# One quad's weight loads on ScalarE's queue, loads and casts in another order, three loads pinned

## The chip, the cores and the metric

The kernel runs on one core of one Trainium2 chip. The metric is the device time in microseconds of one execution. The core has five engines with an instruction stream each: TensorE (PE in the profile, with its weight loads as PEld), VectorE (DVE), ScalarE (ACT), GpSimd (POOL) and SyncE (SP). SP here does nothing but issue DMAs; POOL and ScalarE can issue DMAs among their other work. A DMA's data are moved by the core's 16 DMA engines.

## The reference

```python
def reference(x, w1, w2):          # x 8 x 1024 x 1024, w1 1024 x 4096, w2 4096 x 1024, all float32
    h = x @ w1
    h = 0.5 * h * (1 + np.tanh(np.sqrt(2 / np.pi) * (h + 0.044715 * h ** 3)))
    return (h @ w2).astype(np.float32)
```

It is two matrix products with a gelu between them.

## The kernel before

The 8192 rows of x are taken as eight superblocks (numbered 0 to 7) of 1024 rows. In each, `g = gelu(x w1)` is computed and kept on the chip in float16, and then `g w2`.

Each of the two products is done by Strassen's method in Winograd's form: operands are cut into 2 x 2 blocks named "11", "12", "21", "22", seven products of blocks or of sums of blocks are computed instead of eight, and the results are added up. In superblocks 2 to 7 the method is used on two levels, so that one of the seven products is itself seven smaller ones. Products are numbered 1 to 7. Those of the weights that are plain blocks are 1, 2 and 3 (`W_TERM`); 5, 6, 7 and 4 are sums (`SUMS`). Names like "s7" are the inner sums of product 7.

**Superblocks 0 and 1** make the weights ready for all others. `matmul1` (L531) multiplies with one level, from `MadeQuad` objects (L189), each a quarter of w1's columns. In superblock 0 a quad is cast from w1 and written to DRAM (`w1_d`, L115). In superblock 1 it is loaded back from `w1_d` in four loads of 512 KB (L198, blocks 12, 11, 22, 21), and its sums are made on DVE (`sum`) and stored by POOL (L243). `product` (L501) calls `multiply` (L496), whose matmuls carry L497. `matmul2_made` (L840) does the second product, with matmuls at L1124, and makes, splits and stores w2's blocks and sums (`w2_d`, `in_d`). At the end of superblock 0's call it also transposes x's next superblock by DMA (`x_transpose`, L482, 16 transposes on SP, shown as L162), stores w2's block 22 (`keep("22")`, four stores on SP) and makes superblock 1's first `MadeQuad`.

**Superblocks 2 to 7** run `matmul1_late` (L774) and `matmul2` (L1142).

- `matmul1_late` goes through eight iterations j (called pairs) of 11.1 us, with an order of work written out by hand (`PAIR`, L30); its matmuls carry L712. A pair's weights come from a `StoredHalf` (L268): one load of 512 KB for each entry of `GROUPS` (L27, the loads carry L284), each holding two things that lie side by side in DRAM, for example products 1 and 5 together, or product 7 with its inner sums.
- The same loop brings in the next superblock's rows of x. In pairs 0 to 3 `x_cast_paced` (L475) has POOL copy a few elements of the current g (the "pace" copy, L477) and then issue two DMAs (L472) that cast 128 rows each from float32 to float16 in DRAM. In pairs 4 to 7 SP issues four DMA transposes each: blocks "22" and "21" (rows 512 to 1023) first, then "12" and "11" (rows 0 to 511).
- `matmul2` takes the seven products one after another as `Inner` objects (L1017), in the order 4, 1, 2, 5, 6, 7, 3 (L1194). Its matmuls carry L1082. Each `Inner` loads seven pieces of w2 (`load`): raw pieces from `w2_d` (L1038) and inner sums from `in_d` (L1034). Near the end, at products 7 and 3, the next superblock's first two `StoredHalf` objects are made, and their loads go out.

**What sets the order.** A scheduler places instructions on each engine. Matmuls, most copies and sums and a part of the DMAs are pinned (`keep_in_program_order`, for DMAs through `load_in_order`, L161) and keep the order of the program among each other. An unpinned load may be placed earlier, as soon as its tile is free. All loads from DRAM and the transposes stand in one queue, SP's, and what waits there holds up what is behind it. Most of them use tiles of the pool `up` (24 buffers); the tile names `mu` (pool `mp`, 2 buffers) and `xi` (one buffer) are two others, which come free at other times. SP's DMAs signal through eight completion counters in turn, so a DMA is issued only once the one eight places before it has landed.

Of the kernel before, what the change touches and what calls it, by code (L numbers as in the profile page):

```python
# [23 lines left out]
SUMS = tuple(W_SUM)  # L24
BLOCKS = ("11", "21", "12", "22")
STEPS = (1, 2, 6, 5, 7, 3, 4)
GROUPS = ((1, 5), ("s1", "s5"), (2, "s2"), (7, "s7"), (3, "s3"), (6, 4))  # L27
MADE_HALF = 3
ROOM = (("11", 4), ("11", 8), ("11", 12), ("22", 4), ("22", 8), ("22", 12), ("21", 4), ("21", 8), ("21", 12))
PAIR = """  # L30
m26' h41' z31' q1' r1' x77 v0' m11 s1' m15 x35 x36 z22' u1' X57' c1 m36' m35' m32' X76' m51 e30'
# [41 lines left out]
def kernel(  # L73
# [7 lines left out]
    nc = tc.nc  # L81
# [19 lines left out]
    up = ctx.enter_context(tc.tile_pool(name="up", bufs=24))  # L101
    gp = ctx.enter_context(tc.tile_pool(name="gp", bufs=1))
    gcp = ctx.enter_context(tc.tile_pool(name="gcp", bufs=4))
    mp = ctx.enter_context(tc.tile_pool(name="mp", bufs=2))
    xip = ctx.enter_context(tc.tile_pool(name="xip", bufs=1))
# [11 lines left out]
        for q in range(NI // QC)  # L117
        for n, ks in enumerate(GROUPS + (("12",),))
    }
    in_d = {m: dram.tile([P, 4, NI // 2, OH // 2], DT, name=f"in_d{m}") for m in range(1, 8)}  # L120
# [5 lines left out]
    term = {b: m for m, b in W_TERM.items()}  # L126
# [7 lines left out]
    def unit(rows, cols):  # L134
        return up.tile([P, rows, cols], DT, name="u")
# [6 lines left out]
    def w1_at(q, key):  # L142
        for (at, ks), d in w1_d.items():
            if at == q and key in ks:
                return d[:, :, ks.index(key), :]
# [4 lines left out]
    def halves(t):  # L150
        return t.rearrange("p (h k) n -> p h (k n)", h=2)
# [9 lines left out]
    def load_in_order(out, in_, **kw):  # L161
        return tc.keep_in_program_order(nc.sync.dma_start(out=out, in_=in_, **kw))  # L162
# [26 lines left out]
    class MadeQuad:  # L189


        def __init__(self, q, first, store):
            self.q, self.first, self.store = q, first, store
            self.raw = {b: unit(2 * KH, 2 * P) for b in BLOCKS}
            self.ops = {m: self.raw[b] for m, b in W_TERM.items()}
            if not first:
                for b in ("12", "11", "22", "21"):
                    nc.sync.dma_start(out=halves(self.raw[b]), in_=w1_at(q, term.get(b, b)))  # L198

        def load(self):  # L200

# [66 lines left out]
    class StoredHalf:  # L268


        def __init__(self, i, room=()):
            q, h = divmod(i, 2)
            self.ops, self.sums = {}, {}
            self.room = list(room)
            for ks in GROUPS:
                two = None
                if ks != ("s1", "s5"):
                    two = self.two(ks)
                    if ks == (1, 5):
                        self.both = two  # L280
                elif 0 < i < MADE_HALF:
                    two = self.two(ks)
# [75 lines left out]
    def x_blocks():  # L358
        return {b: unit(KH, HT) for b in ("22", "21", "12", "11")}
# [107 lines left out]
    def x_cast(s, after, rows=range(0, SB, P), xb=None):  # L467
        if xb is None:
            xb = xdram.tile([SB, H], DT, name="xb")
        with tc.issue_after(after.ins):  # L470
            for q in rows:
                nc.gpsimd.dma_start(out=xb[q:q + P, :], in_=x2[s * SB + q:s * SB + q + P, :])  # L472
        return xb

    def x_cast_paced(s, g_chunk, q, xb, pin=False):  # L475

        mark = nc.gpsimd.tensor_copy(out=pace, in_=g_chunk[:, :2])  # L477
        if pin:
            tc.keep_in_program_order(mark)
        return x_cast(s, mark, range(q * P, (q + 2) * P, P), xb)  # L480
# [293 lines left out]
    def matmul1_late(xs, sb, quads, g):  # L774
        n = NI // 2
        nxt = {}
        early = Inner(4, g["22"])
        made = set(xs.inner)
        last = None
        for j in range(n + 1):  # L780
            if j < n:
                quads += [StoredHalf(i) for i in range(len(quads), min(j + 3, n))]
                now = Pair(j, quads[j], xs, g)
            for key in PAIR:
                late = key.count("'")
                key = key.rstrip("'")
                if key[0] in "xX":
                    if late == j and int(key[1]) not in made:
                        xs.inner_sum(int(key[1]), int(key[2]), nc.vector if key[0] == "x" else nc.gpsimd)
                elif key == "b":  # L790
                    if 4 <= j < n:
                        early.make_quarter(7, j - 4)
                elif key[0] == "r":
                    if j == n - 1 + late:
                        early.make_quarter(6, int(key[1]))
                elif key[0] == "k":
                    if MADE_HALF <= j + 1 < n:
                        quads[j + 1].make(int(key[1]))
                elif late:
                    for i in BEGIN.get(key, ()) if j == n else ():  # L800
                        early.begin(i)
                    if last is not None:
                        last.run(key)
                elif j < n:
                    now.run(key)
            last = now
            if j == n:
                break
            if j == n - 1:
                early.load(STEPS[:3])  # L810
            if sb < NSB - 1:
                if j < 4:
                    nxt["xb"] = x_cast_paced(sb + 1, g["22"][:, 2 * j, :], 2 * j, nxt.get("xb"), True)
                if j == 3:
                    nxt["blocks"] = x_blocks()
                if j > 3:
                    x_transpose(nxt["xb"], load_in_order, nxt["blocks"], range(j - 4, j - 3))
        blocks = nxt.get("blocks")
        return g, early, None if blocks is None else XOps(blocks)
# [20 lines left out]
    def matmul2_made(sb, g, keep_w1, xb):  # L840
# [24 lines left out]
        def keep(b):  # L865
            if sb == 0:
                for q in range(NI // QC):
                    load_in_order(w2_at(q, term.get(b, b)), raw[b][q])
# [19 lines left out]
        s2, a, p5, t6, at = {}, {}, {}, {}, {}  # L888
# [47 lines left out]
        for m, name, first in (  # L936
            (1, "a", True), (2, "b", True), (5, "c", True), (6, "a", False),
            (3, "c", False), (7, "a", False), (4, "a", False),
        ):
            for q in range(NQ):  # L940
                if first:
                    banks[name].append(psum())
                bank = banks[name][q]
                matmuls2(bank, s2[q] if m == 6 else rows(g[operands[m]], q), pieces(m), first)
                post(m, q, bank)
                if (m, q) == (5, 0) and sb == 0:
                    xb = x_cast(sb + 1, nc.gpsimd.tensor_copy(out=pace, in_=p5[0][:, :2]))
                if (m, q) == ((5, 0) if sb else (6, NQ - 1)):
                    xs = XOps(x_transpose(xb, load_in_order))
                    keep("22")  # L950
                if (m, q) == (3, NQ - 1) and sb == 0:
                    quad = MadeQuad(0, False, True)
                if (m, q) == (4, 0) and sb:
                    quad = StoredHalf(0)
                if (m, q) == (1, NQ - 1) and sb == 0:
                    sums[5] = [unit(2, HALF) for _ in range(NI // QC)]
                    for t in sums[5]:
                        act_copy(t[:, 0, :1], warm)
                    bring("22", act_copy, True)
                    keep("21")  # L960
                    keep("12")
                run((m, q))
# [54 lines left out]
    class Inner:  # L1017
# [7 lines left out]
        def load(self, steps=STEPS):  # L1025
            for j in steps:
                if j in self.y:
                    continue
                pool, name = {(3, 3): (mp, "mu"), (3, 4): (xip, "xi")}.get((self.m, j), (up, "u"))
                self.y[j] = pool.tile([P, NI // 2, OH // 2], DT, name=name)  # L1030
                if j in W_TERM:
                    self.load_raw(j)
                else:
                    nc.sync.dma_start(out=self.y[j], in_=in_d[self.m][:, SUMS.index(j)])  # L1034

        def load_raw(self, j):
            k, b = (int(d) - 1 for d in W_TERM[j])
            nc.sync.dma_start(  # L1038
                out=self.y[j].rearrange("p c n -> p (c n)"),
                in_=w2_d[k, self.m][:, b].rearrange("p h n -> p (h n)"),  # L1040
            )
# [100 lines left out]
    def matmul2(sb, g, early, nxt):  # L1142
# [55 lines left out]
        for m, after in zip(order, order[1:] + (None,)):  # L1198
# [3 lines left out]
            if m == 7 and not end:  # L1202
                new.update({b: g_tile(b) for b in ("11", "22")})
                quads.append(StoredHalf(0, room(new, ROOM[:5])))
            elif m == 3 and not end:
                new["21"] = g_tile("21")
                quads.append(StoredHalf(1, room(new, ROOM[5:])))
            if m in (6, 3):
# [16 lines left out]
    for sb in range(NSB):  # L1225
        if sb < 2:
            g, nxt = matmul1(xs, sb, quads, first if sb == 0 else None)
            xs, quads = matmul2_made(sb, g, None if sb else quads[-1].keep_raw, nxt)
            continue
        g, early, nxt = matmul1_late(xs, sb, quads, g_late or g_tiles())  # L1230
# [32 lines left out]
```

## Time and profile before

| | us |
|---|---|
| time, median of 3 runs | 1462.79 |
| lowest and highest | 1462.77, 1466.14 |
| the profiled execution's own time | 1462.57 |
| its span | 1460.8 |
| PE busy | 1450.4 |
| DVE busy | 1211.2 |
| ScalarE busy | 681.1 |
| POOL busy | 620.8 |

The span is the time from the first to the last thing that the profiler saw; 1.77 us of the execution lie around it. "Busy" is the time in which an engine executes; waits and the issuing of DMAs are not in it. In the profile's rows "out<-in" names the tiles written and read, with buffer numbers left out, and L with a number is a line of the kernel. SPq is the issuing of DMAs by SP. "DMA share" is the mean busy share of the 16 DMA engines; it can come out a little above 1 in a short window.

The chain of work that ended last is 87% PE and 7% DMA. DMA moves 472.72 MB in the span, a mean of 324 GB/s, and in most of the 40 slices of the span the DMA engines are busy for nine tenths or more. A load of 512 KB into `u` from `w_d` lands 10.2 us after its issue in the median.

### The profile page before, as it was taken

The numbers are of one execution on the slowest core, as the hardware profiler recorded it, in microseconds if no ns is written. First come the engines' busy times: TensorE is split into PE (matmuls) and PEld (weight loads), VectorE is DVE, ScalarE is ACT, GpSimd is POOL, SyncE is SP. The second block draws the span as 40 slices with busy tenths as digits, with TensorE's granted clock in tenths as the row PEclk, the third lists the DMA queues.
The fourth block names the chain that finished last, engine by engine and source line by source line (L and its number), as shares of the span: only waits on it lengthen the run. The fifth ranks groups of instructions, "written<-read, shape, count | busy, mean of one in ns | idle before, by whom it ended". The sixth has DMA issues, their size and how long they took to land.

```text
span 1460.8 us, 28718 instructions
## 1 busy us (share of the span) xinstructions
PE 1450.4 (99%) x10635; PEld 1039.4 (71%) x10635; DVE 1211.2 (83%) x2029; ACT 681.1 (47%) x1406; POOL 620.8 (42%) x634
## 2 busy tenths in 40 slices
PE   9999999999999999999999999999999999999998
PEld 5444444444467888778877788777887778877887
DVE  5657659748768899889998899988998889988897
ACT  5665116641068611784118831388214872168610
POOL 1442222213359411792128820488005961168411
PEclk9999999999999999999999999999999999999999
DMA  9999999798799999999999999999999989996597
GB/s 322 339 348 383 290 331 358 276 304 259 296 359 272 282 352 366 373 264 337 338 377 370 229 371 336 363 356 225 398 344 362 331 237 389 354 385 231 210 362 265
DMA packets 205709, 472.72 MB, mean 324 GB/s; under 512 B 75648, under 2 KB 80768, under 8 KB 204672
## 3 DMA queue, kind: packets, MB, share of 16 engines
q1 hardware_dynamic: 177632, 373.35, 74.1%
q0 software_dynamic: 27936, 97.53, 22.3%
q8 instruction: 83, 1.36, 0.4%
q14 instruction: 58, 0.48, 0.1%
HBM read 370.15 MB, written 115.34 MB: 332 GB/s over the span
## 4 chain that ended last, share of the span: by engine, by line
PE 87%; DMA 7%; issue 3%; POOL 1%; ACT 0%; SPq 0%; DVE 0%; POOLq 0%; DVEq 0%
PE ps L1082 35%; PE ps L712 23%; PE ps L497 21%; PE ps L1124 7%; DMA gc<-in_w_dram 3%; DMA u<-in_w_dram 2%; DMA w_d<-u 1%; PE ps L430 1%; DMA xb<-in_x_dram 1%; DMA u<-in_d 1%; POOL u L168 0%; POOL out_dram L826 0%; PE ps L407 0%; POOL in_d L979 0%; ACT u L165 0%
## 5 line engine op out<-in xcount | busy, mean ns | idle before, releaser
L165 ACT COPY tmp<-ps 128x512 f32<-128x512 f32 (+1 forms) x536 | 268.8, 540 | 313.3 <-PE ps L497 168.2
L497 PE MATMUL ps<-u 128*128 128x512 f16 x1552 | 363.7, 379 | 3.5 <-DMA u<-w_d 2.7
L1082 PE MATMUL ps<-u,gc 128*128 128x256 f16 x2592 | 290.0, 273 | 0.1
L1082 PEld LDWEIGHTS <-gc 128*128 128x128 f16 x2688 | 263.0, 98 | 30.7 <-issue 0.3
L138 DVE TENSOR_TENSOR tmp<-tmp,ps 128x256 f32<-128x256 f32 (+1 forms) x372 | 199.9, 545 | 87.0 <-PE ps L712 29.8
L497 PEld LDWEIGHTS <-u 128*128 128x128 f16 x1552 | 151.7, 98 | 150.6 <-DMA u<-w_d 3.6
L838 POOL DMA_DIRECT2D out_dram<-u x70 | 63.8, 949 | 443.7 <-DVE u L138 220.3
L712 PEld LDWEIGHTS <-u 128*128 128x128 f16 x2026 | 198.2, 98 | 55.4
L138 DVE TENSOR_TENSOR u<-u 128x2048 f16<-128x2048 f16 (+3 forms) x264 | 204.7, 814 | 33.1 <-DMA w_d<-u 12.6
L165 ACT COPY u<-ps 128x512 f32<-128x512 f32 (+1 forms) x134 | 78.0, 587 | 327.6 <-PE ps L1082 319.3
L1082 PE MATMUL ps<-u,g 128*128 128x256 f16 x1920 | 219.4, 273 | 0.0
L712 PE MATMUL ps<-u 128*128 128x256 f16 x1342 | 216.9, 273 | 0.0
L1082 PEld LDWEIGHTS <-g 128*128 128x128 f16 x2016 | 197.3, 98 | 22.8
L510 ACT ACTIVATE g<-tmp 128x512 f16<-128x512 f32 x282 | 174.0, 640 | 52.2 <-DVE tmp L138 51.2
L138 DVE TENSOR_TENSOR ps<-tmp,ps 128x256 f32<-128x256 f32 x444 | 181.3, 426 | 19.4 <-PE ps L712 12.2
L138 DVE TENSOR_TENSOR u<-u,ps 128x512 f32<-128x512 f32 x216 | 147.2, 683 | 25.9 <-PE ps L1082 16.7
L1124 PE MATMUL ps<-u,g 128*128 128x512 f16 x768 | 166.4, 379 | 0.0
L510 ACT ACTIVATE g<-ps 128x512 f16<-128x512 f32 x230 | 137.8, 600 | 24.8 <-PE ps L712 14.6
L1124 PEld LDWEIGHTS <-g 128*128 128x128 f16 x768 | 75.1, 98 | 90.7
L138 DVE TENSOR_TENSOR tmp<-ps,tmp 128x512 f32<-128x512 f32 x126 | 86.7, 690 | 54.2 <-PE ps L497 42.8
L764 POOL TENSOR_TENSOR tmp<-tmp 128x512 f32<-128x512 f32 x96 | 122.0, 1274 | 20.2 <-DVE tmp L138 13.4
L138 DVE TENSOR_TENSOR gc<-g,gc 128x2048 f16<-128x2048 f16 x78 | 95.1, 1219 | 1.3 <-PE ps L1082 1.3
(70 smaller groups left out, 1506.4 us busy)
## 6 DMA issues: line engine op xcount, KB each, us to landing
u<-w_d SPq DMA_DIRECT2D x347, 512.0 KB, 10.2
u<-in_d SPq DMA_DIRECT2D x162, 512.0 KB, 10.3
out_dram<-u POOLq DMA_DIRECT2D x70, 512.0 KB, 11.1
gc<-in_w_dram SPq DMA_DIRECT2D x48, 512.0 KB, 6.0
g<-w_d SPq DMA_DIRECT2D x45, 512.0 KB, 13.2
w_d<-u POOLq DMA_DIRECT2D x40, 512.0 KB, 7.1
w_d<-u SPq DMA_DIRECT2D x32, 512.0 KB, 8.9
xb<-in_x_dram POOLq DMA_DIRECT2D x56, 256.0 KB, 7.5
```

Of the source, the lines that this page charges most:

```text
L138: i = nc.vector.tensor_tensor(out=out, in0=in0, in1=in1, op=op)
L165: tc.keep_in_program_order(nc.scalar.copy(out=out, in_=in_))
L430: tc.keep_in_program_order(nc.tensor.matmul(bank[:, cols], lhsT=w[:, k, :], rhs=self.xs.blocks[f"{a}{r}"][:, k, cols], start=r == 1 and k ...
L497: tc.keep_in_program_order(nc.tensor.matmul(bank, lhsT=w, rhs=x, start=first and k == 0, stop=k == n - 1, skip_group_check=not first,))
L510: gelu_last[0] = nc.scalar.activation(out=out, in_=src, func=GELU, scale=scale)
L712: tc.keep_in_program_order(nc.tensor.matmul(out, lhsT=w, rhs=x, start=first and k == 0, stop=k == 1, skip_group_check=not first,))
L764: tc.keep_in_program_order(nc.gpsimd.tensor_tensor(out=t, in0=t, in1=temp("p", m), op=ADD))
L838: return nc.gpsimd.dma_start(out=rows, in_=src, **kw)
L1082: tc.keep_in_program_order(nc.tensor.matmul(bank[:, i * OH // 2:(i + 1) * OH // 2], lhsT=t[:, c, i * P:(i + 1) * P], rhs=self.y[j][:, c, : ...
L1124: tc.keep_in_program_order(nc.tensor.matmul(pair(bank), lhsT=a[:, c, :], rhs=chunks(pieces[c // QC])[:, :, c % QC, :], start=(first and c ...
```

## The change

1. In `MadeQuad`, the four loads of the quad with q = 0 are issued by ScalarE; those of the other quads remain on SP. Only superblock 1's first quad is concerned, since superblock 0's quads are not loaded this way.
2. In `GROUPS`, (7, "s7") stands before (2, "s2"), and (6, 4) before (3, "s3"). This is the order of a half's loads, and the numbering of the DRAM tiles.
3. x's casts go out in pairs 1 to 4 instead of 0 to 3, with rows 512 to 1023 first (`CAST_ROWS`: pair to first block of 128 rows). The pace copy reads chunk 2j - 1 of g's block 22 instead of 2j.
4. In `Inner.load`, the loads of (product, step) (7, 1), (3, 3) and (3, 4) are pinned, the last two being those into `mu` and `xi`.
5. `keep("22")` stands behind the making of superblock 1's first quad instead of ahead of it.

In the built program PE's and DVE's instructions keep their order, and no instruction is added or removed; four DMAs change from SP's stream to ScalarE's.

```diff
-GROUPS = ((1, 5), ("s1", "s5"), (2, "s2"), (7, "s7"), (3, "s3"), (6, 4))
+GROUPS = ((1, 5), ("s1", "s5"), (7, "s7"), (2, "s2"), (6, 4), (3, "s3"))
 MADE_HALF = 3
+CAST_ROWS = {1: 4, 2: 6, 3: 0, 4: 2}
...
             if not first:
+                queue = nc.sync if q else nc.scalar
                 for b in ("12", "11", "22", "21"):
-                    nc.sync.dma_start(out=halves(self.raw[b]), in_=w1_at(q, term.get(b, b)))
+                    queue.dma_start(out=halves(self.raw[b]), in_=w1_at(q, term.get(b, b)))
...
             if sb < NSB - 1:
-                if j < 4:
-                    nxt["xb"] = x_cast_paced(sb + 1, g["22"][:, 2 * j, :], 2 * j, nxt.get("xb"), True)
+                if j in CAST_ROWS:
+                    nxt["xb"] = x_cast_paced(
+                        sb + 1, g["22"][:, 2 * j - 1, :], CAST_ROWS[j], nxt.get("xb"), True
+                    )
...
                 if (m, q) == ((5, 0) if sb else (6, NQ - 1)):
                     xs = XOps(x_transpose(xb, load_in_order))
-                    keep("22")
                 if (m, q) == (3, NQ - 1) and sb == 0:
                     quad = MadeQuad(0, False, True)
+                    keep("22")
...
             for j in steps:
                 if j in self.y:
                     continue
-                pool, name = {(3, 3): (mp, "mu"), (3, 4): (xip, "xi")}.get((self.m, j), (up, "u"))
+                late = {(3, 3): (mp, "mu"), (3, 4): (xip, "xi")}
+                pool, name = late.get((self.m, j), (up, "u"))
+                dma = load_in_order if (self.m, j) in ((7, 1), *late) else nc.sync.dma_start
                 self.y[j] = pool.tile([P, NI // 2, OH // 2], DT, name=name)
                 if j in W_TERM:
-                    self.load_raw(j)
+                    self.load_raw(j, dma)
                 else:
-                    nc.sync.dma_start(out=self.y[j], in_=in_d[self.m][:, SUMS.index(j)])
+                    dma(out=self.y[j], in_=in_d[self.m][:, SUMS.index(j)])
...
-        def load_raw(self, j):
+        def load_raw(self, j, dma):
             k, b = (int(d) - 1 for d in W_TERM[j])
-            nc.sync.dma_start(
+            dma(
```

## The prediction

> **What bounds the kernel now.** I read the page first, then PE's table of waits, then the timelines of all engines where PE waited.
>
> ```profile
> span 1460.8 us, 28718 instructions
> PE 1450.4 (99%) x10635; PEld 1039.4 (71%) x10635; DVE 1211.2 (83%) x2029; ACT 681.1 (47%) x1406; POOL 620.8 (42%) x634
> ...
> PEclk9999999999999999999999999999999999999999
> ...
> PE ps L497 <- DMA u<-w_d: 2.7, 2, 1.9
> ...
> PE ps L497 <- DVE tmp L138: 0.8, 1, 0.8
> ```
>
> PE is busy for all but 10.4 us, at a granted clock that is in the top tenth in each slice. The other engines matter only where they make PE wait. About 5 us of the idle time are the start and 4 the tail (last matmul 1456.8), which the change does not touch. The waits table has two rows in the part that it does touch: 2.7 us for loads into u from w_d, and 0.8 us for DVE. PE's timeline shows where they lie:
>
> ```profile
> 211.33 1.90 PE L497 MATMUL ps<-u 128*128 128x512 f16 x8 [1.87 <-DMA u<-w_d]
> 214.02 10.53 PE L497 MATMUL ps<-u 128*128 128x512 f16 x48 [0.79 <-DMA u<-w_d]
> 225.40 0.81 PE L497 MATMUL ps<-u 128*128 128x512 f16 x3 [0.84 <-DVE tmp L138]
> ```
>
> This is the start of superblock 1's first matmul. The three gaps are 1.87 + 0.79 + 0.84 = 3.50 us; counted from start to start of the matmuls at their 216 ns, where the modelled ends drop out, 4.0 us. One more gap of 0.30 us is at 1201.37. So all that can be won is 4.3 us, 0.29% of the time. Elsewhere PE runs back to back, and the change can only lose.
>
> What the gap at 211.33 waits for is seen on the queues of SP, ScalarE and DVE (start, length, instructions; in brackets the idle time before and its releaser):
>
> ```profile
> 197.34 3.59 SPq L162 DMA_DIRECT2D w_d<-u  x4
> 201.04 39.98 SPq L198 DMA_DIRECT2D u<-w_d  x12
> ...
> 199.14 0.59 ACT L165 COPY tmp<-ps 128x512 f32<-128x512 f32 x1 [30.49 <-PE ps L1124]
> ...
> 211.38 12.17 DVE L138 TENSOR_TENSOR u<-u 128x2048 f16<-128x2048 f16 x24 [4.70 <-DMA u<-w_d]
> ```
>
> SP issues four stores of a w2 block and only then, from 201.04, the quad's four loads (201.04, 202.39, 203.63, 204.70). They land at 209.95, 211.28, 212.63 and 213.97: 9 us after issue, 1.33 us apart. The second (block 11) is what PE's first product and DVE's first sum wait for, the fourth (block 21) what PE waits for at 214.02.
>
> **Part 1: the first quad's loads on ScalarE's queue.** Nothing is removed: four issues leave SP, four enter ScalarE. In ScalarE's built order they stand between the copy of 168.06 and that of 199.14, in 30.49 us of idle time, so the issuing itself (0.3 us where a queue is free, 0.97 in the median of L198, 1.24 at most) is hidden. Their data were written long before. What holds them is that each waits for an earlier DMA whose completion counter it takes over: four of the last transposes of x, which landed at 196.7, 199.8, 200.0 and 201.2. So they issue at about 196.7, 199.8, 200.5 and 201.2, against the four times above: 4.3, 2.6, 3.1 and 3.5 us earlier. The second decides: DVE's start and PE's first product both need it, so I take **2.6 us**. Landing at 208.7 it is there when the last matmul before ends (209.46), and the first gap goes; the fourth would land at about 211.4 (1.33 us spacing behind the third), about when PE asks for it; the third gap depends on DVE, which starts 2.6 us earlier as PE does, so it stays. Upper bound: all 4.0 us. Lower bound: nothing, if the landings are set by the bytes ahead and not by the issue (first rival). I stay near the issue times, because the engines' time here holds few bytes: 200 GB/s from 194 to 198, against 394 from 210 to 214.
>
> The share of DMA in these windows is 1.25, 1.05, 1.04, 1.06 and 1.04, so the engines are taken throughout. The Trainium skill (DMA: Bandwidth & Descriptors, "Issuing engines are not separate DMA queues") says that starting DMAs from several engines saves only the issuing time, since all run on the same 16 engines; by that, this part would come to about 0. The same page ("Queues, rings and completion order") has each DMA engine turn from one queue to the next after a packet; by that the loads would not wait behind SP's stores. No trace here has plain loads on ScalarE's queue, so neither is shown.
>
> Queued behind the loads on ScalarE is the copy of 199.14. If the fourth load waits until 201.2, the copy comes up to 3 us late. Its reader is an output store on POOL (200.02); its bank is next written after 210; and the three copies behind it, 3.45 us apart with 2.87 us idle each, take the delay up in one step. Cost 0. If the loads slow SP's four stores (landing 202.2 to 208.6), DVE's sums that overwrite those tiles come later; the last is only needed within the 24 sums from 211.38, so some 3 us of cover.
>
> **Part 2: the groups.** The halves' loads of products 7 and 2, and of (6, 4) and 3, change places. Each load is 512 KB before and after, so each tile shifts by one slot (1.28 us) and now comes in the order in which PE first reads it (7, 2, 6, 3). Gain 0, as PE does not wait there; it helps against part 4.
>
> **Part 3: casts in pairs 1 to 4.** The same eight casts (256 KB, 7.5 us to landing) go out one pair of 11.1 us later. The transposes of rows 512 to 1023 come in pairs 4 and 5, those of rows 0 to 511 in pairs 6 and 7; as rows 512 to 1023 are now cast first, each has over 6 us to spare. Cost 0. The pace copy no longer waits for a gelu (2.34 us in the one at 589.49); POOL only. What matters: at the start of a superblock the casts shared the DMA engines with first loads (share 1.18 at 592 to 596), and one gap between landings was 3.9 us (594.91 to 598.81) instead of 1.27. So 2.6 us of queue are given back exactly there.
>
> **Part 4: three pinned loads.** Before, the scheduler hoisted product 3's two loads (`mu` at 1181.00 and `xi` at 1192.77 in superblock 6, read by PE from 1278 on) some 85 us ahead of use:
>
> ```profile
> 1181.00 0.37 SPq L1038 DMA_DIRECT2D mu<-w_d  x1
> ...
> 1189.43 0.52 SPq L284 DMA_DIRECT2D mu<-w_d  x1
> 1192.77 0.32 SPq L1034 DMA_DIRECT2D xi<-in_d  x1
> 1193.14 1.70 SPq L1034 DMA_DIRECT2D u<-in_d  x2
> ...
> 1259.86 2.85 SPq L1034 DMA_DIRECT2D u<-in_d  x3
> 1263.68 8.99 SPq L284 DMA_DIRECT2D g<-w_d  x6
> ```
>
> Now these two, and the next superblock's `mu` load seen at 1189.43, issue after the three of 1259.86. Three loads at about 1.27 us leave one end and enter the other: 3.8 us. Where they leave, the load issued at 1193.14 landed 8.2 us later, at 1201.3, and PE's 0.30 us gap followed: it goes, **-0.3**. Where they enter, I put the loads in their new order into the landing times of before, slot by slot, and set each against the first matmul that reads it: the two themselves keep 0.2 us (superblock 6) to 3.5 us. The next superblock's first weights come 3.8 us later, less 2.6 from part 3, less up to 1.2 from part 2. In the same table, with part 2 but no relief from part 3, the worst load at the five starts after superblocks 2 to 6 is short by 0.1, 0.2, 1.3, 1.9 and 0, together 3.5 us; with it, 0; with landings another 2 us later and no relief, about 13. I take **+0.5**: nearer to the row with relief, because the casts' gap is measured just there.
>
> **Part 5: block 22's stores** are issued after the quad is made; this leaves SP's order as it was: 0.
>
> **Sum.** -2.6 - 0.3 + 0.5 = -2.4 us on the profiled execution's 1462.57 (span 1460.8 and 1.77 around it): 1460.2. The median shown is 0.22 above that execution, so **1460.4**.
>
> **Rivals.**
> *The queue buys nothing.* For: the share above 1 throughout, and landings 1.33 us apart, the pace of a full set of engines. Eight transfers at 1.33 us take 10.6 us in any order. Against: transposes moved only 200 GB/s. Then -0.3 + 0.5: about 1463.
> *All gaps go.* If the loads also overtake the stores, the fourth lands by 210 and DVE starts early enough: -4.0 - 0.3: 1458.5. Against: DVE must gain more than PE.
> *The pinned loads starve the next superblock* (the other side). Place: the first products after each of superblocks 2 to 6, five boundaries. For: slack there is 0.04 to 2.7 us already in the load of 1193.14 and its like, and landing takes 12.4 us of queue at 1258.60. Against: the cast pair is gone from there. It decides once the stalls exceed the 2.9 us won, 0.6 us a boundary; with 13 us it is 1472.7, with about 8 us 1468.
> *The pinned order changes nothing,* because the waits on tiles, not the scheduler, set the issue: the built order shows the three in their new places, so I give it no chance of its own.
>
> **Chances.** Forecast 0.50 (1458.5 to 1462.5), no gain 0.17, all gaps 0.10, starving 0.23. About 0.3%, 4.4 us, is what can be told from no change: faster means below 1458.4, which needs more than the gaps hold: 0.06 for noise and the bounds. Slower means above 1467.2: 0.18 of the starving case's 0.23. Within: 0.76. The range, 1458.2 to 1468.5, leaves out some 0.04 below and 0.13 above.
>
> **What would show it.** Right: four L198 loads on ScalarE from about 197, no gap at 211, one under 0.5 us near 211.4, DVE's 24 sums from about 208.8, about 0.8 us left near 223; no gap near 1201; PE back to back at the start of each superblock. Wrong: landings still at 210 to 214; PE waiting in L712 for w_d loads in the first pair of superblocks 3 to 7, or in L1082 for `mu` or `xi`; transposes late in pairs 4 to 7; ScalarE's copy near 199 held so long that PE waits for a bank.

## The result, and the profile after

| | median us | executions | ratio to the kernel before, 95% interval |
|---|---|---|---|
| kernel before, beside it | 1462.78 | 8 (1459.31 to 1471.88) | |
| changed kernel | 1473.65 | 8 (1467.52 to 1479.63) | 1.0069 [1.0044, 1.0093] |

The change makes the kernel 0.7% slower. The forecast was 1460.4, a little faster, and the range ended at 1468.5.

The profiled execution of the changed kernel took 1468.39 us, 5.8 more than that of before. It is the second fastest of its eight, so about 5 of the 10.9 us between the medians are in no trace. Its page and PE's table of waits (line waited for: sum, times, longest) have:

```profile
span 1466.6 us, 28750 instructions
...
PE ps L499 <- ACT tmp L166: 5.4, 4, 2.1
```

Both rows of waits of before are gone: PE no longer waits for loads into `u`, nor for DVE at 225. A new one has come, four waits for a copy on ScalarE. (The changed kernel's lines are numbered 1 to 6 higher.) To see where the 5.8 us are, I compared the start of each matmul in both traces; PE's order is the same, so the difference between the two is flat wherever neither stalls:

| stretch | change of the difference, us |
|---|---|
| start of the kernel | +0.48 |
| 209 to 225 | -3.61 |
| superblock 2 | 0 |
| superblocks 3, 4, 5, each 28 us in | +1.07, +1.69, +2.51 |
| superblock 6, 28 us in | +3.94 |
| 1201 | -0.29 |
| superblock 7 | 0 |

So the gaps at 211 went and four stalls came, all at the same place of the order by hand, in pair 2 (28 us is counted from a superblock's first matmul; the expectations below say 27). The one of superblock 6 can be followed from engine to engine. POOL's timeline of before, then of the changed kernel (start, length, instructions; idle time before and its releaser):

```profile
1130.34 1.16 POOL L315 TENSOR_TENSOR mu<-u 128x512 f16<-128x512 f16 x1 [1.17 <-DVE ps L138]
1131.45 1.27 POOL L764 TENSOR_TENSOR tmp<-tmp 128x512 f32<-128x512 f32 x1
```

```profile
1128.18 1.27 POOL L766 TENSOR_TENSOR tmp<-tmp 128x512 f32<-128x512 f32 x1 [3.17 <-DVE tmp L139]
1135.86 1.15 POOL L317 TENSOR_TENSOR mu<-u 128x512 f16<-128x512 f16 x1 [6.41 <-DMA u<-w_d]
1136.96 1.26 POOL L766 TENSOR_TENSOR tmp<-tmp 128x512 f32<-128x512 f32 x1
```

L317 (L315 before) is `StoredHalf.make`: for halves from number 3 on, the inner sums of products 1 and 5 are not loaded but made on POOL, from the half's first load. That load landed at 1135.69, and POOL had been idle for 6.41 us. Behind the sum, in POOL's order, stands L766, a sum of products (`v1` in the order by hand), which has nothing to do with the load.

In the kernel before POOL waited for this load too. The load landed at 1130.22, and the sum began at 1130.34; in superblocks 3 to 7 of both kernels it begins 0.12 to 0.17 us after the landing. The row of before names DVE, whose update came 0.05 us after the landing, but the sum follows the landing as it does everywhere else. POOL's wait, from 1127.3 for 2.945 us, is in the view of L315:

```profile
L315 POOLq EVENT_SEMAPHORE  x1: 2945/2945/2945, 1127.3 to 1127.3; - x1
```

ScalarE and PE in the changed kernel:

```profile
1138.26 0.58 ACT L166 COPY tmp<-ps 128x512 f32<-128x512 f32 x1 [3.69 <-POOL tmp L766]
```

```profile
1138.89 1.21 PE L499 MATMUL ps<-u 128*128 128x512 f16 x4 [2.10 <-ACT tmp L166]
```

ScalarE's copy waits for L766, and PE for the bank that the copy empties. The chain is load, POOL's sum, the sum behind it, copy, matmul; PE's own weights are not in it. Before, the copy followed the sum in the same way:

```profile
1132.75 0.59 ACT L165 COPY tmp<-ps 128x512 f32<-128x512 f32 x1 [0.32 <-POOL tmp L764]
```

But the same matmul started only at 1134.50, 4.28 us after the landing. In the changed kernel, where PE waits for the chain, 3.20 us lie between the two (1135.69 and 1138.89). So the load had about 1.1 us to spare there, all of it behind POOL's sum.

### The profile page after: what moved, and what is told of

Its sections match the earlier page's. It is cut to its first block, busy times and chain, and to the rows that moved or that the text cites. A ratio compares the mean times of both kernels' runs of the same rounds, so it can differ in the third digit from the quotient of the medians.

```text
span 1466.6 us, 28750 instructions
## 1 busy us (share of the span) xinstructions
PE 1453.3 (99%) x10635; PEld 1039.7 (71%) x10635; DVE 1210.9 (83%) x2029; ACT 680.4 (46%) x1406; POOL 619.0 (42%) x634
## 4 chain that ended last, share of the span: by engine, by line
PE 87%; DMA 10%; SPq 1%; POOL 1%; DVE 1%; ACT 1%; issue 0%; POOLq 0%; DVEq 0%; ACTq 0%
PE ps L1088 31%; PE ps L499 23%; PE ps L714 21%; PE ps L1130 11%; DMA g<-w_d 4%; DMA u<-w_d 3%; DMA mu<-w_d 2%; DMA gc<-in_w_dram 1%; PE ps L432 1%; SPq L163 1%; DMA u<-xb 0%; PE ps L409 0%; ACT tmp L166 0%; DMA u<-in_x_dram 0%; POOL tmp L766 0%; POOL mu L317 0%
## 5 line engine op out<-in xcount | busy, mean ns | idle before, releaser
L499 PE MATMUL ps<-u 128*128 128x512 f16 x1472 | 344.5, 380 | 6.4 <-ACT tmp L166 5.4
L714 PE MATMUL ps<-u 128*128 128x256 f16 x1372 | 222.0, 273 | 0.2
L766 POOL TENSOR_TENSOR tmp<-tmp 128x512 f32<-128x512 f32 x96 | 121.8, 1271 | 45.0 <-DVE tmp L139 30.3
L714 PE MATMUL ps<-gc,mu 128*128 128x256 f16 x504 | 96.2, 273 | 0.0
```

The costliest lines, as they stand in the source:

```text
L499: tc.keep_in_program_order(nc.tensor.matmul(bank, lhsT=w, rhs=x, start=first and k == 0, stop=k == n - 1, skip_group_check=not first,))
L714: tc.keep_in_program_order(nc.tensor.matmul(out, lhsT=w, rhs=x, start=first and k == 0, stop=k == 1, skip_group_check=not first,))
L766: tc.keep_in_program_order(nc.gpsimd.tensor_tensor(out=t, in0=t, in1=temp("p", m), op=ADD))
```

## The experiments

The line of thought after the result: part 4's three loads make half 3's first load late, and POOL's fixed order carries that to PE. The rival was part 3, the casts, which POOL issues in the same pair. Ratios below are to the kernel before run on the same chip (medians of 1459.5 to 1461.1 us in these). "Stalls" are the four in superblocks 3 to 6.

**Part 4 undone (e1).** The three loads unpinned, the rest as changed.

```diff
-                dma = load_in_order if (self.m, j) in ((7, 1), *late) else nc.sync.dma_start
+                dma = nc.sync.dma_start
```

> The changed kernel with the three loads of part 4 unpinned again; parts 1, 2, 3 and 5 stay. Theory (late weights on POOL): the changed kernel loses about 9 us in superblocks 3 to 6, 27 us into each, because POOL's first sum for half 3 waits for that half's first load, and a sum that ScalarE and PE need stands behind it on POOL; the load is late because of the three loads that part 4 puts ahead of it. Then the four stalls go, the 3.6 us won at 211 stay, and the time is about 3 to 4 us below the kernel before (ratio 0.997 to 0.998). Rival (the casts): the pace copy and the casts of part 3 in pair 1 are what makes POOL late; then the stalls stay at 1 to 2.4 us each and the time is 4 us or more above the kernel before.

Measured: 1460.19 us, ratio 1.0005 [0.998, 1.003]; profiled execution 1457.92 with no stall after 225. The rival falls: casts and pace copies are where the changed kernel has them. The forecast gain of 3 to 4 us is in this trace, the fastest of twelve executions, but not in the median.

**POOL's order (e2).** All loads as in the changed kernel; `k7`, POOL's first sum of a half, behind `v1` (only the part of the line that changes is shown).

```diff
-x15 k7 m22' z23' v1'
+x15 m22' z23' v1' k7
```

> The changed kernel with one step of the order by hand moved: POOL's first sum of a half stands behind the sum v1 that ScalarE waits for, instead of ahead of it. All loads are as in the changed kernel. Theory (POOL's order): POOL still waits for half 3's first load, but nothing that PE needs soon stands behind it; the four stalls of 1.1 to 2.4 us go, and the time is about 3 to 4 us below the kernel before (ratio 0.997 to 0.998). Rival (PE itself lacks weights, or the casts): the stalls stay, ratio 1.003 or more. Between: the sums of half 3 come late for PE, and a shorter stall appears one pair later.

Measured: 1458.36 us, 0.9989 [0.9964, 1.0015], no stall. POOL's timeline:

```profile
1124.06 1.27 POOL L766 TENSOR_TENSOR tmp<-tmp 128x512 f32<-128x512 f32 x1 [0.69 <-ACT tmp L166]
1129.39 1.16 POOL L317 TENSOR_TENSOR mu<-u 128x512 f16<-128x512 f16 x1 [4.06 <-DMA u<-w_d]
```

POOL still waits 4.06 us for the load; the sum that ScalarE needs has gone ahead. In three of the four superblocks the load is later than in the changed kernel (table below), and it costs nothing. This is the cause shown by its link rather than by its source. With the same loads the ratio goes from 1.0069 to 0.9989, and the intervals are apart, so the loss of the median hangs on this order too, not only the part of it that the trace shows.

**Part 4 alone (e4)** on the kernel before.

> The kernel before with part 4 alone: casts still in pairs 0 to 3, groups in the old order, first quad on SP. Theory (late weights on POOL): stalls 27 us into superblocks 3 to 6, at least as long as in the changed kernel (9 us together or more), and perhaps further ones in pair 0 where the casts stand ahead of first loads; ratio 1.005 to 1.010. Rival (the casts of part 3 are the cause): no stall at 27 us, at most the 3.5 us of my table in the first pairs; ratio 0.9995 to 1.002.

Measured: 1473.35 us, 1.0086 [1.0052, 1.012]: as slow as the whole change. The place differs from what was expected:

```profile
PE ps L497 <- DMA u<-w_d: 7.1, 4, 2.5
PE ps L497 <- ACT tmp L165: 2.7, 1, 2.7
```

With the casts in pairs 0 to 3, PE itself lacks weights, in three of the four superblocks 15 us in, in pair 1, and only superblock 4 shows POOL's stall. So neither side had the place. Waiting on a superblock's early weights is what the prediction's rival named, though it named the first pair, and this is the second. Parts 2 and 3 (1 and 5 touch only superblock 1) moved the shortage 13 us on, from PE's loads to POOL's.

**One of the three back early (e6)** (the load into `xi`; a part of the line).

```diff
-in ((7, 1), *late) else
+in ((7, 1), (3, 3)) else
```

> The changed kernel with one of the three loads back in its early place (the load into xi); the other two stay late. Theory (bytes ahead of half 3's first load): 1.27 us less stands ahead, each of the four stalls of 1.1, 1.7, 2.5 and 2.4 us falls by about 1.3 us, to 0, 0.4, 1.2 and 1.1 us, and none is long enough to touch the clock; ratio 1.000 to 1.002. Rival (pinning as such holds SP's queue up, not the number of loads): stalls as before, ratio 1.004 to 1.009.

Measured: 1466.64 us, 1.0041 [1.0023, 1.0059]. The loss shrinks from 0.69% to 0.41%, but the intervals overlap, and 1.0041 lies in the rival's range, not in the theory's. In the traces the first gaps of the stalls in superblocks 4 to 6 fell by 0.56, 0.98 and 1.51 us, and that of superblock 3 rose by 1.13; the half clock described at the end is gone, and the four stalls together come to 6.1 us instead of 9.2. That the loss goes down with one load less is what these traces suggest; 1.3 us for each load is not shown.

**Casts in pairs 2 to 5 (e5).**

```diff
-CAST_ROWS = {1: 4, 2: 6, 3: 0, 4: 2}
+CAST_ROWS = {2: 4, 3: 6, 4: 0, 5: 2}
```

> The changed kernel with x's casts one pair later still, in pairs 2 to 5, so that none goes out ahead of the landing of half 3's first load; all loads and POOL's sums stay. Theory (bytes ahead of half 3's first load): two casts of 256 KB leave, about 2.6 us at the landing pace of before, so that load lands some 2.6 us earlier, against a lateness that gave stalls of 1.1, 1.7, 2.5 and 2.4 us; the first two go, the others fall below 0.5, ratio about 0.999 to 1.001. If transposes come late instead, SP waits in pair 4 and PE in pairs 6 or 7. Rival (the load is late for its place on SP's queue and the completion counters, whatever the casts do): the stalls stay as they were, ratio 1.004 to 1.009.

Measured: 1474.59 us, 1.0095 [1.0062, 1.0128]. The stalls in pair 2 did go: their first gaps are 0, 0.64, 0 and 0 us where the changed kernel has 0.58, 1.20, 2.01 and 2.26. But the transposes now end later, and behind them on SP are the loads of product 4. SP and PE in superblock 6:

```profile
1194.93 1.30 SPq L1044 DMA_DIRECT2D u<-w_d  x2
```

```profile
1200.56 1.04 PE L1088 MATMUL ps<-u,g 128*128 128x256 f16 x4 [3.92 <-DMA u<-w_d]
```

The casts do hold the load up, but later they hold up something else. The waits came in the second matrix product, not in pairs 6 or 7.

How late half 3's first load is, from the traces: its landing less the start of one matmul of pair 2, the same in all kernels, in superblocks 3 to 6 (us):

| kernel | sb 3 | sb 4 | sb 5 | sb 6 |
|---|---|---|---|---|
| before | -2.10 | -1.94 | -1.13 | -1.35 |
| changed | +0.31 | +0.93 | +1.78 | +2.00 |
| part 4 undone | -1.82 | -2.05 | -0.86 | -1.39 |
| POOL's order (no stall) | +1.16 | +1.62 | +2.26 | +1.62 |
| one load back | +1.44 | +0.37 | +0.80 | +0.47 |
| casts 2 to 5 | -1.38 | +0.37 | -0.69 | -0.26 |

The changed kernel has it 2.4 to 3.4 us later than the kernel before, of the 3.8 us that three loads take. Wherever PE stalls in pair 2 in the changed kernel, with one load back and with casts in pairs 2 to 5, its first gap is the table's number plus 0.23 to 0.28 us. By that the load had 0.9 to 1.8 us to spare in the kernel before, and PE waited for what came beyond it.

**The queue alone (e3)** (parts 1 and 5 on the kernel before).

> The kernel before with parts 1 and 5 alone. Both theories: the three gaps at 211 to 225 go as in the changed kernel, 3.6 us, and nothing else changes: ratio 0.9975, 1459 us where the kernel before takes 1462.8. If the queue were also a part of the loss, the stalls at 27 us into superblocks 3 to 6 would be seen here too.

Measured: 1462.36 us, 1.0009 [0.9982, 1.0037]. The gain is not there. PE in this profiled execution:

```profile
209.08 1.89 PE L498 MATMUL ps<-u 128*128 128x512 f16 x8
214.15 18.05 PE L498 MATMUL ps<-u 128*128 128x512 f16 x75 [3.18 <-DMA u<-w_d]
```

The loads were issued on ScalarE from 197.76. The second landed at 208.43, 2.9 us earlier than before, and the gap at 211 is gone; but the fourth landed at 214.10 against 213.97 before, and PE waits for that one.

**The queue undone (e7)** in the version with POOL's order changed (parts 1 and 5 out).

> The kernel of the run e2 (the sum first) with parts 1 and 5 undone: the first quad's loads are on SP again, behind the four stores. Theory (the queue buys nothing, the DMA engines' bytes set the landings): where the transposes end near 197 there is no gap at 211, where they end near 201 there is one of 2 to 4 us, with either queue; the time is that of e2 within 0.1%, about 1458 to 1461. Rival (my forecast): 2.6 to 3.6 us more than e2, ratio to the kernel before 1.001 or more where e2 had 0.999.

**POOL's order on the kernel before (e8).**

> The kernel before with POOL's first sum of a half behind the sum v1, and nothing else. Theory: half 3's first load landed only 0.12 us ahead of that sum in superblock 6 before, so in some executions it is late there too; with the sum first these stalls go, the median falls by up to 2 us, and the spread above 1465 us shrinks. Rival (the slow executions of the kernel before come from elsewhere, the gap at 211 or the starts of superblocks): median and spread as before, ratio 0.999 to 1.001.

Measured: 1461.75 us, 1.0016 [0.9993, 1.0038], for e7, and 1460.63 us, 1.0005 [0.9984, 1.0027], for e8. By its numbers e7 meets the rival (3.4 us above e2, 1.0016 where e2 had 0.9989) and not the theory; but the two intervals overlap, so it decides little. e8 meets its rival as well: on the kernel before, POOL's order gains nothing. Its profiled execution, of 1468.42 us, shows where the time of a long execution goes. PE's timeline and SP's:

```profile
217.43 14.88 PE L497 MATMUL ps<-u 128*128 128x512 f16 x59 [8.72 <-DMA u<-w_d]
```

```profile
166.69 37.99 SPq L162 DMA_TRANSPOSE u<-xb  x16
204.73 3.60 SPq L162 DMA_DIRECT2D w_d<-u  x4
```

The 16 transposes ahead of the loads took SP 38.0 us to issue, where part 4 alone, its first quad also on SP, has them in 25.9:

```profile
167.50 25.93 SPq L162 DMA_TRANSPOSE u<-xb  x16
193.48 3.70 SPq L162 DMA_DIRECT2D w_d<-u  x4
```

and there the first quad has no gap at 211 at all. In the traces, the landing of the last transpose against what PE lost at the three gaps together (start to start, without stretches of half clock, us):

| loads on | last transpose landed: lost |
|---|---|
| SP | 196.7 (e4): 1.0; 197.4 (e11): 1.9; 201.2 (before): 4.0; 203.7 (e7): 5.3; 208.5 (e8): 9.2 |
| ScalarE | 196.3 (e1): 0; 197.7 (changed): 0.4; 197.7 (e6): 0.6; 198.1 (e2): 0; 198.2 (e5): 0; 200.7 (e3): 3.3; 207.7 (e12): 6.3 |

The loss goes with the landing of the transposes; why that varies from one execution to the next no run shows. Take what PE lost here, half clock included, off the profiled times of the eight versions without stalls (before, e1, e2, e3, e7, e8, e11, e12): 1457.6 to 1458.6 us are left, where the times themselves run from 1457.9 to 1468.4. So nearly all of the spread between these traces is made here.

The queue is worth 1 to 2 us at the same landing, 3 at the latest ones, as far as so few traces tell. The medians don't show it: 1460.4 for the versions with ScalarE's queue and no stalls (e1, e2, e3, 36 executions), 1460.6 for those with SP's (the kernel before beside them, e7 and e8, 82 executions).

**Earlier casts for superblock 1**, so that its transposes can start earlier: on the kernel before, and on the changed kernel with part 4 undone and POOL's order changed; first 14 us earlier (e9, e10), then 5 (e11, e12).

```diff
-                if (m, q) == (5, 0) and sb == 0:
-                    xb = x_cast(sb + 1, nc.gpsimd.tensor_copy(out=pace, in_=p5[0][:, :2]))
+                if (m, q) == (2, 0) and sb == 0:
+                    xb = x_cast(sb + 1, nc.gpsimd.tensor_copy(out=pace, in_=a[q][:, :2]))
```

(with `(2, NQ - 1)` for the later place)

> The kernel before with one thing moved: the eight casts of superblock 1's rows go out after the first quarter of product 2 instead of the first of product 5, some 14 us earlier. Theory (the gap at 211 and most of the spread of times come from the transposes, which end between 196 and 208 us from one execution to the next, and not from the queue of the loads behind them): the transposes start earlier, the gaps at 211 to 225 go in nearly all executions with the loads still on SP; the median falls to about 1458 and the executions above 1464 us, a quarter of those of the kernel before, become rare; ratio 0.996 to 0.999. Rival (the spread comes from elsewhere): median and spread as before. Against both: the casts now stand in the way of w2's last blocks, and PE waits in the first matmul2 near 145 to 200.

> The changed kernel with part 4 undone, POOL's sum v1 first, and the early casts of the run e9. Theory: no stall is left between 20 and 1450 us; time 1457.5 to 1458.5 us, no slower than the kernel before and 12 to 15 us faster than the changed kernel; against e9 no difference, since parts 1, 2 and 3 buy nothing once the transposes are early. Rival (part 1's queue matters for itself): 1 us or more faster than e9.

Measured: 1.004 [1.0021, 1.0059] and 1.0024 [1.0007, 1.0041], slower: the theory fell, and what was named against it came. The gaps at 211 to 225 are gone in both traces, in e9 with the loads on SP and the last transpose at 193.8; but PE also comes there 8.0 and 5.7 us later than before, which alone would hide a gap of 4 us. e10's median is 1.4 us below e9's, as its rival had it, with intervals that overlap. The casts now hold up w2's last blocks (a load of w2 issued at 131.22 landed 23.3 us later, where before such a load took 10 to 12), and PE waits in superblock 0's second product; the run on the kernel before:

```profile
156.87 1.02 PE L1124 MATMUL ps<-u,gc 128*128 128x512 f16 x4 [2.26 <-DVE u L138]
159.43 1.68 PE L1124 MATMUL ps<-u,gc 128*128 128x512 f16 x4 [1.53 <-DVE u L138]
```

> The kernel before with the eight casts of superblock 1's rows behind the last quarter of product 2, some 5 us earlier than before and 10 us later than in e9. Theory (transposes set the gap at 211): the transposes end some 3 us earlier, so the gap at 211 is gone in most executions, and the casts come late enough to spare the waits of e9 at 155; median near 1458 to 1459. Rival (what is gained at 211 is paid at 155 wherever the casts stand): waits in the first matmul2 near 155 of 1 to 3 us, time 1460 to 1464.

> The changed kernel with part 4 undone, POOL's sum v1 first, and the casts of e11. Theory: as e11 within 0.1%, and 0.8 to 1% faster than the changed kernel, since the three early loads are back; a version at or a little below the kernel before. Rival: parts 1 to 3 cost something of their own, and this is slower than e11 by 1 us or more.

Measured: 1460.12 us, 1.0002 [0.9985, 1.0019], and 1460.40 us, 1.0001 [0.998, 1.0022]; the 1458 to 1459 us of e11's theory were not reached. There are no waits at 155, but the transposes still vary: in e12's trace the last one landed at 207.74 and PE lost 1.77 and 4.23 us at 211 and 217. No version clearly beats the kernel before; the lowest median is that of POOL's order, whose interval still holds 1.

## Why the prediction was wrong, step by step

**Part 4 is the step that failed.** Its late loads were put at +0.5 us; in the changed kernel's trace they cost 9.2 us (1.7 of them by the clock, below). "Set each against the first matmul that reads it" left out every reader that is not a matmul. The table showed PE's slack at the starts of superblocks as enough, and with part 3's relief it was: in the changed kernel's trace PE never waits for a load there. But half 3's first load is read first by POOL, and POOL waited for it already in the kernel before (landing 1130.22, sum at 1130.34): at this reader there was no slack at all. Behind it, POOL's next sum, the copy and the bank had 0.9 to 1.8 us to spare, and the load became 2.4 to 3.4 us later. Those rows could be read before the change was run.

**The relief was put in the wrong place.** "2.6 us of queue are given back exactly there" holds for PE's weights early in a superblock, where part 4 alone makes PE wait and the changed kernel does not. For half 3's first load it does not hold: with part 4 undone, and parts 2 and 3 in, that load lands 0.1 us earlier to 0.3 us later than before (table). In superblock 6 one pair of casts is then issued between its issue and its landing (1117.20), where before it was two (1114.47 and 1126.86); this gave back nothing. And part 2 regroups only what comes behind the first two loads of a half.

**Rival 3 had the sign, the condition and the size** ("with 13 us it is 1472.7, with about 8 us 1468"; its own sum makes the first 1472.9), but placed the wait at PE's first products, and held 0.23 of the chance.

**Part 1.** The first gap went, and what sets the issue was read rightly: in the changed kernel the four loads issue at 191.49, 195.33, 196.19 and 197.77, each 0.1 us after one of the last transposes has landed. That is 3.4 to 5.2 us earlier than forecast, because the transposes ended earlier, and this trace shows 3.6 of the 4.0 us of the gaps won. By that trace alone "all gaps go" would nearly have been confirmed. The runs show that much of it was the luck of that execution: where the transposes end as early with SP's queue, only 1.0 to 1.9 us are lost. "The second decides" failed in e3: the second load came early, the fourth did not, which fits the eight transfers that must pass in any order. The pooled medians side with the first rival, "the queue buys nothing"; the table leaves room for 1 to 3 us, and e7 against e2 for 3.4. What part 1 is worth stays open. By the Trainium skill ("DMA: Bandwidth & Descriptors", "Issuing engines are not separate DMA queues") only issuing time is saved; the landing of 214.10 against 213.97 agrees. The rule of turns between queues, in the same page ("Queues, rings and completion order"), fits that the second load came 2.9 us sooner and SP's last store 5.7 us later (214.34 against 208.62).

**Parts 2, 3 and 5** cost nothing that these runs can tell, as forecast: with part 4 undone the ratio is 1.0005 [0.998, 1.003]. **The 0.30 us at 1201** went, but it also went in e3 and e8, which have no part 4: it too comes and goes with the execution.

**The bound.** "Elsewhere PE runs back to back, and the change can only lose" was right: part 4 touched only places of that kind. The three times shown of before hid its spread, 0.9% in eight executions; the gap at 211, which cost 4.0 us in one trace and 9.2 in another, is a part of it.

## What to carry to other kernels

When a load is moved, list its readers on all engines, and what is queued behind each reader; the slack that counts is the smallest of these, and on an engine with a fixed order a late operand stalls work that never touches it. A reader that starts 0.12 us after the landing already waits for it, whatever its row names as the releaser. Where a sum can be moved behind the one that others wait for, the same late load costs nothing. And a gap of 2 us in one trace is not yet a gap of the kernel: look whether what feeds it varies from one execution to the next before counting on it.

## What the runs showed that I had not expected

A stall can cost more than itself. In superblock 6 of the changed kernel the granted clock fell after the wait of 2.3 us, counted from start to start (stretch, length, all in us, PE busy, then the other engines, granted clock, DMA share, GB/s):

```profile
1138.00:1142.00 4.00, 3.11 (x12) 1.60 (x12) 2.47 (x6) 3.63 (x8) 4.00 (x5) 0.70 1.03 412
```

It was halved for 3.413 us, which costs 1.7: that is why superblock 6 lost 3.94 us. Such stretches in the other traces last 3.413 or 6.827 us, after PE waits of 2.3 to 8.9 us; but waits of 2.7, 2.8 and 3.3 us were not followed by one. The full-speed stretches between are whole multiples of 3.413 us, for example 204.8, and when a grid of that step is laid over each trace, the clock fell when PE was idle (start to start) for 2.18 us or more of one step, and not at 2.12 or less. The Trainium skill ("TensorE: Matmul & The Clock Gate", Part 1) tells of a free-running window of 3413 ns and half clock after an idle one. The step agrees, but 64% of a window idle (2.18 us) was enough here.
